# Stick-breaking attention on one core: the score product of the low key parts over 128 rows instead of 64

## The chip, the core and the metric

The kernel runs on one core of one Trainium2 chip. The time is device microseconds from start to end of one execution, lower is better. All five engines take part: TensorE (PE, with its weight loads PEld) does the matrix products, VectorE (DVE) and ScalarE (ACT) the elementwise work, GpSimd (POOL) sets memory and issues some transfers, SyncE (SP) issues most transfers.

## The reference

A small decoder trunk over 512 positions of width 1024: an S5 state-space mixer with a gated output (GLU), a gated feed-forward layer with a width-3 convolution, one shared key/value projection, a stick-breaking attention of 16 heads of 64 dimensions over those keys and values, a second feed-forward layer, and a last norm. The part that the change touches is this:

```python
def stick_breaking_attention(h, w_q, k, v, w_o):
    scale = HEAD_DIM ** -0.5
    q = (h @ w_q).reshape(...).transpose(0, 2, 1, 3) * scale
    for blk in range(seq // Q_BLOCK):
        ...
        z = jnp.einsum('bhqd,bhkd->bhqk', qb, kb).astype(jnp.float32)
        causal = s_idx < t_idx
        log_beta = jax.nn.log_sigmoid(z)
        log_one_minus = jnp.where(causal, log_beta - z, 0.0)
        rem = lax.cumsum(log_one_minus, axis=3, reverse=True) - log_one_minus
        w = jnp.where(causal, jnp.exp(log_beta + rem), 0.0)
        outs.append(jnp.einsum('bhqk,bhkd->bhqd', w, vb))
    return o @ w_o
```

## The kernel before

The trunk runs in stages, one after the other: S5 with its GLU, the first feed-forward layer, attention, the second feed-forward layer with the last norm. Activations lie with features on the 128 partitions and the 512 positions along the row. Every 32-bit operand of a large product is split into a high part that TensorE's rounded 32-bit format (fp32r) holds and a low part, the rest; a product is then three matmuls, high by high, high by low, low by high. Weights come in by DMA as raw tiles (`awr` in attention, `wvr` in the GLU), get their high part on ScalarE (`awh`, line 157) and their low part on VectorE (`awl`, line 112).

In attention the keys and queries of two heads at a time are one 128-row tile: rows 0 to 63 are the even head, rows 64 to 127 the odd head. `Proj` makes for the keys the tiles `kqa` and `kqb`, one for each head, that hold the head's high part twice (rows 0 to 63 and rows 64 to 127), and one tile `kql` with the low parts of both heads, each on its own rows. For the queries, `kqa` and `kqb` hold the high part on the head's own rows and the low part on the other 64. So the first score matmul of a block of 128 keys, `kqa` by `kqa`, sums high by high and high by low over 128 rows. The second, low keys by high queries, takes 64 rows of `kql` and of the queries: `kl[rows, kc]`, `qs[rows, q]`.

`Head.scores` goes through the key blocks 3, 1, 2, 0, which reach 128, 384, 256 and 512 queries. The scores `z` fill three PSUM banks. After the block's two matmuls a product of the identity with a mask tile adds -1e30 above the diagonal: over 256 columns after block 1 (for the diagonals of blocks 3 and 1, which share a bank), over 128 columns after blocks 2 and 0. That is 11 matmuls for a head. A head then goes on so: ScalarE makes the log terms `t`, VectorE the softplus and its split `lh`, `ll`; TensorE adds the running sums (`cumulate`: products with `cntri` and `cnones`); ScalarE exponentiates to `wh` and `w`, VectorE makes `wl` from them; TensorE multiplies by the values `vv` into `ob`.

The loop over the 16 heads is written out in the order in which PE, DVE and ACT run it (`tc.manual_schedule`): `cumulate` of head i, `scores` of head i+1, a third of the projection jobs (`kqb`, `v`, `ob` products that prepare later heads or the output), `values` of head i, then two more thirds of the jobs. Between them DVE and ACT run the splits of weights and keys. Outside the loop the scheduler of the language orders the instructions, GpSimd's for the whole program among them. Tiles come from rings: `kq` is a ring of ten tiles, five for each pair of heads, thus two pairs. Memory of closed pools is used again, and an instruction on a new tile waits for the last use of what lay there.

The convolution's coefficients of each feed-forward layer are loaded to a tile of their own (`cw`, line 818, issued by ScalarE).

Of the kernel before, what the change touches and what calls it, by code (L numbers as in the profile page):

```python
# [7 lines left out]
F32 = mybir.dt.float32  # L8
F32R = mybir.dt.float32r
# [38 lines left out]
def trunk(ctx: ExitStack, tc: tile.TileContext, A, out):  # L48
# [11 lines left out]
    class Work:  # L60
        """The work tiles [128, 512] of a phase, by tag."""

# [13 lines left out]
    def banks_by_tag(**bufs):  # L76
        """Deals the eight banks of PSUM to a phase's tags, those longest unused first."""
        ids = sorted(range(8), key=lambda i: max([n for n, u in enumerate(used) if u == i], default=-1))
        cur["p"] = {}
        for tag, n in bufs.items():  # L80
            cur["p"][tag], ids = ids[:n], ids[n:]
# [37 lines left out]

    # ------------------------------------------------------------ constants  # L120
    par = const.tile([P, 168], F32, name="par")
# [11 lines left out]

    # ------------------------------------------------------------ weights
    def load_raw(src, cols, name="w", dma=None):
# [4 lines left out]
    def load_split(src, cols, gain=None, name="w", dma=None):  # L140
        """src: a [128, cols*128] block of weights in DRAM; two parts whose sum it is exactly."""
        raw = load_raw(src, cols, name, dma)
        if gain is not None:
            i, ks = gain if isinstance(gain, tuple) else (gain, slice(0, KT))
            g = cst[:, i, ks]
            n = ks.stop - ks.start
            r3 = raw.rearrange("p (k n) -> p k n", k=n)
            tt(r3, r3, bc(g, 2, [P, n, 8 * P // n]), MUL)
        return split_w(raw, cols, name)
# [23 lines left out]

    # ------------------------------------------------------------ norms
    def split_x(k, gain, perm=False):
# [63 lines left out]

    # ------------------------------------------------------------ S5  # L240
    def s5(st_next):
        banks_by_tag(st=1, u=2, g=2, kb=1, v=1, y=1)
        with tc.tile_pool(name="s5", bufs=1) as sp, ExitStack() as wctx:
# [59 lines left out]
            def steps():  # L303
                """The steps of the tensor engine that go between the dependent ones."""
                for n in range(KT):
# [30 lines left out]
            def load(k):  # L336
                """Two steps' weights of the first of the gated outputs."""
                raw = wp.tile([P, 8 * P], F32, tag="raw", name="wvr", bufs=3)
                for i in range(0, HALVES, 2):
                    GP.dma_start(out=raw[:, i * 2 * P:(i + 2) * 2 * P].rearrange("p (h c) -> p h c", h=2),  # L340
                                 in_=A["w_glu"][i // 2, :, :, k * P:(k + 2) * P].rearrange("h p c -> p h c"))
                raws.append(raw)
# [127 lines left out]

            # powers 0..8 of A
            pw3 = L("pw3", [32, 3, 9])
# [13 lines left out]

            # the powers times f, which stands with C
            pwc3 = L("pwc3", [32, 3, 8])
# [19 lines left out]

            # unit rotations over the chunks and the decay of a chunk
            mg2 = op2(mag, mag, MUL)  # L510
# [23 lines left out]
            def rotations():  # L534
                """The rotations of the first half of the chunks, of all groups, by doubling."""
                for lv in range(5):
# [13 lines left out]
            def turn_products(n):  # L550
                """The second half of the chunks, of four pairs of groups."""
                q = T("tq", tag="tq").rearrange("p (i r q c) -> p i r q c", i=2, r=2, q=4)
# [13 lines left out]
            def products(m3, pw3, n, e0):  # L566
                """The three products of a complex multiplication by the powers from e0, of four pairs of groups."""
                pr = slice(4 * n, 4 * n + 4)
# [6 lines left out]
            def sums(o, k3):  # L575
                """Their sums: the real part and the (for C negated) imaginary part."""
                o4 = o.rearrange("p (r a c) -> p r a c", r=2, a=4)
                tt(o4, bc(k3[:, :, 0], 1, [P, 2, 4, P]), k3[:, :, 1:3].rearrange("p a t c -> p t a c"), ADD)

            def op_c(n):  # L580
                """C A^e (re, im) of four pairs of groups."""
                k3 = products(c3, pwc3, n, 0)
# [4 lines left out]
            def kk(n):  # L587
                """The within-chunk response, as a matrix from the inputs to the outputs of a chunk."""
                cmr, cmn = unit[n]["c"]
# [24 lines left out]
            def op_b(n):  # L614
                """A^(8-j) bb of four pairs of groups."""
                unit[n] = {}
# [28 lines left out]
            def decays(n):  # L645
                """The decay of a chunk, for the chunks of four pairs of groups after their first."""
                decay[n] = sp2.tile([P, 256], F32, name="mt", bufs=1)
# [4 lines left out]
            def states(n):  # L652
                """The states before each chunk: a real recurrence in the frame that turns with them."""
                pr = slice(4 * n, 4 * n + 4)
# [154 lines left out]

    # ------------------------------------------------------------ conv FFN  # L810
    def ffn(layer, prev, st_next):
# [5 lines left out]
    def ffn_body(layer, xs, rb, st_next):  # L817
        cw = const.tile([P, FT, 4], F32, name=f"cw{layer}")
        nc.scalar.dma_start(out=cw, in_=A["conv"][layer])
# [34 lines left out]

    # ------------------------------------------------------------ attention
    def attention(prev, st_next):
        with Work("att", aw=9, tw=4, os=16, o=2, kq=10, kv=2):
            banks_by_tag(z=6, d0=1, d1=1)
# [4 lines left out]
    def attention_body(ap, xs, rb, rtok, st_next):  # L863
        consts = {}

        def load_consts():
            for n, wd in (("ntri", P), ("nones", P), ("ident", P), ("mask", 2 * P)):
                raw = T("cr", tag="kv")
                nc.scalar.dma_start(out=raw[:, 0:wd], in_=A[n])
                consts[n] = t = ap.tile([P, wd], F32R, name="c" + n)  # L870
# [7 lines left out]

        # the weights, in the order of their use
        class Weight:  # L880
# [23 lines left out]
        class Proj:  # L904
            """Keys or queries of two heads."""
            halves = 2
# [14 lines left out]
            def top(self):  # L921
                """Keys: [high, high] of each head and the low parts; queries: [high, low] and [low, high]."""
                self.a, self.d = T("kqa", F32R, "kq"), T("kqb", F32R, "kq")
# [3 lines left out]
            def rest(self):  # L927
                if self.keys:
                    self.l = T("kql", F32R, "kq")
                    low = self.l[:64], self.l[64:]  # L930
                else:
# [10 lines left out]
        class Vals:  # L942
            """Values of four heads and half of the keys: [keys, block, head, hi|lo], hi and lo swapped for the odd heads."""

# [42 lines left out]
        class Out:  # L987
            """Part of the sum of one output tile, added to the trunk; its steps end at the given ks."""

# [26 lines left out]

        kq, vvs, vws = {}, {}, {}
        width = {0: 512, 1: 384, 2: 256, 3: 128}
        place = {0: (2, 0), 3: (0, 0), 1: (0, 128), 2: (1, 0)}
        banks = ((512, (3, 1)), (256, (2,)), (512, (0,)))  # L1020

        class Head:
# [11 lines left out]
            def scores(self):  # L1034
                keys, queries = kq[self.pair]
                kd, kl, qs, rows = keys[self.e], keys[2], queries[self.e], self.rows
                self.z = [B(f"z{i}", "z") for i in range(3)]
                for kb in (3, 1, 2, 0):
# [3 lines left out]
                    mm(o, kd[:, kc], qs[:, q], kb != 1, False)  # L1042
                    mm(o, kl[rows, kc], qs[rows, q], False, False)
                    if kb == 1:
                        mm(self.z[0][:, 0:2 * P], consts["ident"], consts["mask"], False, False)
                    elif kb != 3:
                        mm(o[:, 0:P], consts["ident"], consts["mask"][:, 0:P], False, False)

            def log_terms(self, between=None):
                """exp, ln of the softplus (ScalarE)."""  # L1050
                self.L = [(W2("lh", wd), W2("ll", wd)) for wd, _ in banks]
# [108 lines left out]

        # which weights are split beside which half of which job
        side = {(j, h): [] for j in range(-2, len(jobs)) for h in range(2)}

        def split_at(m, js, h):
            """Gain a half before, the high part at this half, the low part a half later."""
            p = 2 * js + h
# [166 lines left out]

    # ------------------------------------------------------------ the trunk
    class Next:
# [8 lines left out]
    class Final:  # L1344
        """The last norm: the sums of squares by a product with ones, the last tile and the output by halves."""

# [136 lines left out]
```

## Time and profile before

| | us |
|---|---|
| median of 3 runs | 1259.54 (1258.92 to 1259.91) |
| span of the profiled execution | 1258.9 |
| PE busy in it | 1231.0 (98%) |
| DVE busy | 810.5 (64%) |
| ACT busy | 541.1 (43%) |
| POOL busy | 22.1 (2%) |
| the stretch from the first score block to the end of the last running sums | 608.5 to 850.6 |

The span runs from the first to the last instruction of the profiled execution; it is 0.64 us under the median of the runs. The granted TensorE clock was 0.995 over the span. A matmul's row gives its start and its duration up to the modelled end; since matmuls overlap in the pipeline, what one costs in a stream is the time from its start to the start of the next. Line 106 is the helper that issues every matmul, so that groups are told apart by their tiles.

### The profile page before, as it was taken

How to read it: one execution, taken by the hardware profiler on the slowest of the kernel's cores; microseconds unless marked ns; L12 is line 12 of the kernel's file. 1: busy time of each engine (PE TensorE's matmuls, PEld its weight loads, DVE VectorE, ACT ScalarE, POOL GpSimd, SP SyncE). 2: the span in 40 equal slices, each digit the busy share in tenths (PEclk: the TensorE clock that was granted, in tenths of full speed). 3: DMA queues.
4: the chain of work that ended last, by engine and by line, in shares of the span. 5: the costliest groups of instructions: out<-in, count | busy, mean ns of one | idle time of the engine just before them, and what ended most of it. 6: DMA issues, size and time to landing. Idle time of an engine off the chain costs nothing.

```text
span 1258.9 us, 16218 instructions
## 1 busy us (share of the span) xinstructions
PE 1231.0 (98%) x6411; PEld 987.5 (78%) x6411; DVE 810.5 (64%) x1284; ACT 541.1 (43%) x866; POOL 22.1 (2%) x61
## 2 busy tenths in 40 slices
PE   7989999999999999999999999999999999999996
PEld 3457788788888888888888888888888888888884
DVE  7999664656445635558787878777656345535554
ACT  5235353433223323344676768665433233313331
POOL 1011010000000000000000000000000000000000
PEclk9999999999999999999999999999999999999998
DMA  5565343232233233223211211113333233233321
GB/s 202 148 171 141 102 134 97 87 100 88 97 101 96 88 101 101 97 89 111 68 51 37 65 51 47 39 51 101 101 101 91 94 100 98 88 101 98 94 73 67
DMA packets 55068, 118.54 MB, mean 94 GB/s; under 512 B 12912, under 2 KB 28528, under 8 KB 54992
## 3 DMA queue, kind: packets, MB, share of 16 engines
q1 hardware_dynamic: 50880, 105.55, 27.4%
q0 software_dynamic: 3248, 11.54, 2.9%
q8 instruction: 50, 0.82, 0.3%
q10 hardware_dynamic: 864, 0.42, 0.1%
q14 instruction: 26, 0.21, 0.1%
HBM read 109.10 MB, written 8.39 MB: 93 GB/s over the span
## 4 chain that ended last, share of the span: by engine, by line
PE 90%; DVE 8%; ACT 1%; DMA 1%; issue 1%; SPq 0%; DVEq 0%; ACTq 0%
PE fd L106 19%; PE fu L106 19%; PE fg L106 19%; PE z L106 7%; PE kqb L106 7%; PE gl L106 6%; PE ob L106 5%; PE v L106 4%; DVE k L112 2%; DVE p L112 1%; PE u L106 1%; PE y L106 1%; DVE cm L112 1%; DVE u L112 1%; DVE rv L670 1%
## 5 line engine op out<-in xcount | busy, mean ns | idle before, releaser
L106 PE MATMUL fd<-ah,wdh 128*128 128x512 f32 (+1 forms) x359 | 140.5, 391 | 0.0
L106 PE MATMUL fd<-ah,wdl 128*128 128x512 f32 (+1 forms) x359 | 139.2, 388 | 0.0
L106 PE MATMUL fd<-al,wdh 128*128 128x512 f32 (+1 forms) x359 | 137.8, 384 | 0.0
L112 DVE TENSOR_TENSOR x<-x,fd 128x512 f32<-128x512 f32 (+1 forms) x49 | 33.1, 676 | 119.8 <-PE fd L106 119.8
L157 ACT CAST wuh<-wur 128x1024 fp32r<-128x1024 f32 x44 | 46.4, 1054 | 134.4 <-PE fg L106 118.0
L157 ACT CAST wdh<-wdr 128x896 fp32r<-128x896 f32 (+1 forms) x48 | 47.2, 983 | 127.9 <-PE fd L106 98.1
L112 DVE TENSOR_TENSOR g<-fg,rb 128x512 f32<-128x512 f32 x44 | 30.4, 692 | 96.2 <-PE fg L106 93.5
L106 PE MATMUL fu<-xh,wuh 128*128 128x512 f32 x220 | 86.0, 391 | 0.0
L106 PE MATMUL fg<-xh,wgl 128*128 128x512 f32 x220 | 85.8, 390 | 0.0
L106 PE MATMUL fg<-xh,wgh 128*128 128x512 f32 x220 | 85.7, 390 | 0.0
L106 PE MATMUL fu<-xh,wul 128*128 128x512 f32 x220 | 85.6, 389 | 0.0
L106 PE MATMUL fg<-xl,wgh 128*128 128x512 f32 x220 | 85.6, 389 | 0.0
L106 PE MATMUL fu<-xl,wuh 128*128 128x512 f32 x220 | 85.6, 389 | 0.0
L112 DVE TENSOR_TENSOR u<-fu,rb 128x512 f32<-128x512 f32 x44 | 30.4, 692 | 80.5 <-PE fu L106 80.5
L106 PE MATMUL fu<-xhl,wuh 128*128 128x512 f32 x264 | 81.9, 391 | 0.0
L106 PE MATMUL fg<-xhl,wgh 128*128 128x512 f32 x264 | 81.5, 389 | 0.0
L106 PEld LDWEIGHTS fd<-ah,wdl 128*128 128x128 f32 x359 | 67.4, 188 | 15.2
L106 PEld LDWEIGHTS fd<-al,wdh 128*128 128x128 f32 x359 | 67.4, 188 | 14.8 <-issue 0.2
L106 PEld LDWEIGHTS fd<-ah,wdh 128*128 128x128 f32 x359 | 67.5, 188 | 13.3 <-issue 0.2
L157 ACT CAST wgh<-wgr 128x1024 fp32r<-128x1024 f32 x44 | 46.4, 1054 | 71.0 <-PE fd L106 33.0
L106 PE MATMUL u<-xg,wi 128*128 128x512 f32 x128 | 63.4, 628 | 7.8 <-ACT xg L270 7.8
L109 DVE SCALAR_TENSOR_TENSOR acc<-g,cw,acc 128x511 f32<-128x511 f32 x88 | 65.8, 748 | 2.4 <-ACT acc L832 0.9
(246 smaller groups left out, 2813.1 us busy)
## 6 DMA issues: line engine op xcount, KB each, us to landing
wgr<-in_w_up SPq DMA_DIRECT2D x44, 512.0 KB, 3.5
wur<-in_w_up SPq DMA_DIRECT2D x44, 512.0 KB, 3.5
wdr<-in_w_dn SPq DMA_DIRECT2D x32, 448.0 KB, 3.2
wdr<-in_w_dn SPq DMA_DIRECT2D x16, 512.0 KB, 3.4
wvr<-in_w_glu POOLq DMA_DIRECT2D x12, 512.0 KB, 3.8
ks<-kx SPq DMA_DIRECT2D x32, 128.0 KB, 2.4
m<-ks SPq DMA_DIRECT2D x8, 512.0 KB, 4.1
awr<-in_w_k SPq DMA_DIRECT2D x8, 512.0 KB, 3.5
```

The costliest lines, as they stand in the source:

```text
L106: PE.matmul(o, lhsT=lhsT, rhs=rhs, start=start, stop=stop, skip_group_check=True)
L109: (eng or V).scalar_tensor_tensor(out=o, in0=a, scalar=s, in1=b, op0=op0, op1=op1)
L112: (eng or V).tensor_tensor(out=o, in0=a, in1=b, op=op)
L157: SC.copy(out=hi, in_=raw)
L670: V.tensor_tensor_scan(out=rv[:, c], data0=decay[n], data1=wv[:, c], initial=0.0, op0=MUL, op1=ADD)
```

## The change

The low parts of the keys no longer lie together in one tile of the ring. There are four tiles for the whole stage, `kl00`, `kl01`, `kl10`, `kl11` (128 rows by 512): for two alternating pairs of heads, one tile for each head. Of each tile the head's own 64 rows are written anew for each pair, as before; the other 64 rows are set to zero once, by GpSimd. The second score matmul takes all 128 rows of that tile and of the head's query tile, so that the other rows add nothing. The ring `kq` shrinks from ten tiles to eight. The mask tile is 128 wide instead of 256, and the product over 256 columns reads it twice through an access pattern with a step of zero. The convolution's coefficients of both layers share one buffer. Comments and descriptions in the source are taken out.

```diff
-        cw = const.tile([P, FT, 4], F32, name=f"cw{layer}")
+        cw = const.tile([P, FT, 4], F32, name="cw")
...
-        with Work("att", aw=9, tw=4, os=16, o=2, kq=10, kv=2):
+        with Work("att", aw=9, tw=4, os=16, o=2, kq=8, kv=2):
...
-            for n, wd in (("ntri", P), ("nones", P), ("ident", P), ("mask", 2 * P)):
+            for n, wd in (("ntri", P), ("nones", P), ("ident", P), ("mask", P)):
                 raw = T("cr", tag="kv")
-                nc.scalar.dma_start(out=raw[:, 0:wd], in_=A[n])
+                nc.scalar.dma_start(out=raw[:, 0:wd], in_=A[n][:, 0:wd])
...
                 if self.keys:
-                    self.l = T("kql", F32R, "kq")
-                    low = self.l[:64], self.l[64:]
+                    self.l = lows[self.pair % 2]
+                    low = self.l[0][:64], self.l[1][64:]
...
+        lows = []
+        for i in range(2):
+            pair = [ap.tile([P, S], F32R, name=f"kl{i}{e}") for e in range(2)]
+            for e, t in enumerate(pair):
+                GP.memset(t[64 - 64 * e:128 - 64 * e].bitcast(F32), 0.0)
+            lows.append(pair)
...
-                kd, kl, qs, rows = keys[self.e], keys[2], queries[self.e], self.rows
+                kd, kl, qs = keys[self.e], keys[2][self.e], queries[self.e]
...
                     mm(o, kd[:, kc], qs[:, q], kb != 1, False)
-                    mm(o, kl[rows, kc], qs[rows, q], False, False)
+                    mm(o, kl[:, kc], qs[:, q], False, False)
                     if kb == 1:
-                        mm(self.z[0][:, 0:2 * P], consts["ident"], consts["mask"], False, False)
+                        mm(self.z[0][:, 0:2 * P].rearrange("p (b q) -> p b q", b=2), consts["ident"],
+                           bc(consts["mask"], 1, [P, 2, P]), False, False)
                     elif kb != 3:
-                        mm(o[:, 0:P], consts["ident"], consts["mask"][:, 0:P], False, False)
+                        mm(o[:, 0:P], consts["ident"], consts["mask"], False, False)
```

On PE the order stays. These are the first matmuls of the score block of the second head (the odd one, so that its high keys are `kqb`; sizes are those of the output), before:

```order
L106 MATMUL z_5113<-kqb 128x128
L106 MATMUL z_5113<-kqb,kql 128x128
L106 MATMUL z_5113<-kqb 128x384
L106 MATMUL z_5113<-kqb,kql 128x384
L106 MATMUL z_5113<-cmask,cident 128x256
```

The same place after:

```order
L106 MATMUL z_5119<-kqb 128x128
L106 MATMUL z_5119<-kqb,kl_4763 128x128
L106 MATMUL z_5119<-kqb 128x384
L106 MATMUL z_5119<-kqb,kl_4763 128x384
L106 MATMUL z_5119<-cmask,cident 128x256
```

No matmul has moved; the low keys come from the head's own tile, and the row count of the products, which these rows don't show, is 128 throughout.

On POOL the four instructions that set zeros stand at the end of the S5 stage, between transfers of the GLU's weights (`wvr`); `mt` and `xv` are small tiles of S5:

```order
 L650 MEMSET mt 128x4
 L680 MEMSET xv 128x8
-L137 DMA wvr<-in_w_glu 128x1024 x11
+L137 DMA wvr<-in_w_glu 128x1024
+L1023 MEMSET kl_4762 64x512
+L1023 MEMSET kl_4763 64x512
+L1023 MEMSET kl_4766 64x512
+L1023 MEMSET kl_4767 64x512
+L137 DMA wvr<-in_w_glu 128x1024 x10
```

Ten weight transfers now stand behind the zeros in POOL's queue. By the program's semaphores the first of the four waits for the last use of the memory that the tiles are laid over, on PE the product `yt<-yh,nid` of the last S5 round.

On ACT the load of the second layer's coefficients was the third instruction of the program and now stands near the end of the first feed-forward layer, right after its last Silu (`s<-acc`, line 836).

## The prediction

> **What bounds the kernel now.** I read the page first: the engines' busy time and the chain of work that ended last.
>
> ```profile
> PE 1231.0 (98%) x6411; PEld 987.5 (78%) x6411; DVE 810.5 (64%) x1284; ACT 541.1 (43%) x866; POOL 22.1 (2%) x61
> PE 90%; DVE 8%; ACT 1%; DMA 1%; issue 1%; SPq 0%; DVEq 0%; ACTq 0%
> ```
>
> TensorE carries 90% of the chain. Then the chain in order of time (start, length, what), for the attention stage: its first score block, the running sums and score block of one head, and the running sums of the last head, which has no score block behind it.
>
> ```profile
> 608.53 3.02 PE z L106 x11
> ...
> 622.82 5.68 PE z L106 x29
> ...
> 632.55 5.46 PE kqb L106 x24
> ...
> 658.91 2.92 PE v L106 x24
> ...
> 847.96 2.65 PE z L106 x18
> ```
>
> Between 608.5 and 850.6 the chain is PE alone, one piece after the other without a gap, so in this stage any time that PE saves is saved in the end, until another engine is late. A score block of 11 matmuls takes 3.02 us; 5.68 less 2.65 gives 3.03 for the next one.
>
> Is 3.02 us much for its work? The stream rates are in the same rows: 24 matmuls of 512 columns in 5.46 us, 0.2275 each; 24 of 256 columns in 2.92, 0.1217 each. The timeline of PE (start, duration, what) shows the running sums and then the score block of one head matmul by matmul. The step from start to start is the cost:
>
> ```profile
> 638.08 0.68 PE L106 MATMUL z<-lh,cnones 128*128 128x128 f32 x4
> 638.60 0.40 PE L106 MATMUL z<-ll,cntri 128*128 128x512 f32 x1
> ...
> 640.52 0.22 PE L106 MATMUL z<-kqa 128*128 128x128 f32 x1
> 640.67 0.32 PE L106 MATMUL z<-kqa,kql 64*128 64x128 f32 x1
> 640.92 0.44 PE L106 MATMUL z<-kqa 128*128 128x384 f32 x1
> 641.29 0.43 PE L106 MATMUL z<-kqa,kql 64*128 64x384 f32 x1
> 641.65 0.39 PE L106 MATMUL z<-cmask,cident 128*128 128x256 f32 x1
> 641.88 0.28 PE L106 MATMUL z<-kqa 128*128 128x256 f32 x1
> 642.09 0.38 PE L106 MATMUL z<-kqa,kql 64*128 64x256 f32 x1
> 642.40 0.33 PE L106 MATMUL z<-cmask,cident 128*128 128x128 f32 x1
> 642.56 0.44 PE L106 MATMUL z<-kqa 128*128 128x512 f32 x1
> 642.93 0.50 PE L106 MATMUL z<-kqa,kql 64*128 64x512 f32 x1
> 643.36 0.33 PE L106 MATMUL z<-cmask,cident 128*128 128x128 f32 x1
> 643.53 0.45 PE L106 MATMUL kqb<-xh,awh 128*128 128x512 f32 x1
> 643.81 0.40 PE L106 MATMUL kqb<-xl,awh 128*128 128x512 f32 x1
> ```
>
> The sign to read is 64*128 against 128*128. Every step from a 128-row matmul to a 64-row one and back is long: 0.37 for 512 columns ahead of the switch and 0.43 after it, where 0.2275 is the stream; 0.25 for 128 columns of `kql`. Even the products behind a switch back run late, the mask's (0.23 for 256 columns) and the first `kqb` (0.28). There are eight switches in a block. The running sums just ahead change weights and widths as often, without one switch, and stay near the stream: the four rows merged at 638.08 (three of 128 columns, one of 384) take 0.52, so that at 0.171 for the 384 (three quarters of 0.2275) a 128-column one costs 0.117.
>
> **The change part by part.** The same 11 matmuls stay, all with 128 rows. At the rates above: four of 128 columns at 0.117 (0.468), three of 256 at 0.1217 (0.365), two of 384 at 0.171 (0.342), two of 512 at 0.2275 (0.455), together 1.63 us. Saved per head: 3.02 - 1.63 = 1.39, and 0.05 on the first product behind the block (0.28 against 0.2275), 1.44 in all; times 16 heads, 23.0 us. All of it is on the chain. Two bounds: a block may run at the pure column rate, 3072 columns in 1.36 us, which saves 1.71 a head or 27.4 us; or the extra of the switches may stay whole, which saves nothing. I take 23.0, since the running sums have the same mix of widths.
>
> The TensorE page of the Trainium skill ("TensorE: Matmul & The Clock Gate", Part 3) says that matmuls with few rows overlap when they use distinct row groups, so by it half-height products are the ones to keep; its price is worked out among the rivals. Here each 64-row product stands between two of 128 rows, which use all groups, and the steps above show no overlap.
>
> What is late next? DVE and ACT work for the next head while PE runs on. Their load by stretch of one head (length, then PE, PEld, DVE, ACT, POOL, clock, DMA): the first and the last of the five in which DVE is busy for 13.5 us or more, and one between.
>
> ```profile
> 653.20:668.90 15.70, 15.70 (x111) 14.08 (x110) 13.60 (x22) 11.19 (x23) 0.00 (x0) 1.00 0.22 68
> 684.20:699.40 15.20, 15.20 (x74) 12.16 (x74) 13.56 (x22) 12.44 (x24) 0.00 (x0) 1.00 0.23 71
> 776.00:791.60 15.60, 15.60 (x110) 14.00 (x109) 13.51 (x22) 11.08 (x23) 0.00 (x0) 1.00 0.20 60
> ```
>
> A stretch of 15.20 becomes 13.76, just over DVE's 13.56. The tightest hand-over inside one is that of `wl`, which hangs on the running sums ahead of the score block and is read by the value products behind it:
>
> ```profile
> 690.68 1.62 DVE L112 TENSOR_TENSOR wl<-w,wh 128x512 fp32r<-128x512 f32 x3
> 693.53 0.39 PE L106 MATMUL ob<-wl,vv 128*128 128x512 f32 x1
> 693.50 0.69 DVE L109 SCALAR_TENSOR_TENSOR t<-z,t 128x512 f32<-128x512 f32 x1 [1.20 <-ACT t L1060]
> ```
>
> The last `wl` ends at 692.30 and is read at 693.53, a slack of 1.23; 1.44 less leaves PE waiting 0.21. I charge 0.21 to each of the five heavy stretches, 1 us. DVE's own wait of 1.20 for the log terms says that DVE isn't out of time there. Net gain 22.0.
>
> The zeros: POOL's four MEMSETs of 512 columns. Nearest rows:
>
> ```profile
> 2.47 0.97 POOL L496 MEMSET bdr<- 128x1024 f32 x1
> 3.36 0.97 POOL L497 MEMSET bdi<- 128x1024 f32 x1
> ...
> 151.06 0.53 POOL L137 DMA_DIRECT2D wvr<-in_w_glu  x1 [7.33 <-DVE wvl L112]
> 159.08 0.53 POOL L137 DMA_DIRECT2D wvr<-in_w_glu  x1 [7.49 <-DVE wvl L112]
> ```
>
> ```profile
> 156.31 0.40 PE L106 MATMUL yt<-yh,nid 128*128 128x512 f32 x1
> ```
>
> From start to start 1024 columns take 0.89, so 512 take 0.45 and four 1.8. They may start when `yt<-yh,nid` ends at 156.71 and are over near 158.6, before the next transfer, which VectorE holds back until 159.08 anyway. Cost nothing. If that cover is gone, the ten transfers behind slip, and their own slack is next:
>
> ```profile
> L157 ACT CAST wvh<-wvr x19: 404/1051/1057, 87.1 to 209.8; 128x1024 fp32r<-128x1024 f32 x15, 128x256 fp32r<-128x256 f32 x4
> L137 POOL DMA_DIRECT2D wvr<-in_w_glu x16: 528/528/549, 103.8 to 196.0; - x16
> DMA to landing us min/median/max: 2.9/3.7/5.3
> ```
>
> The last one is issued at 196.0, lands 3.7 later, and its first reader, the cast, starts at 209.8: ten microseconds of cover there. From below: zeros remove no work, so no gain.
>
> The coefficients: one DMA issue less at the start of ACT and one more (0.4) near 549.8, where ACT idles:
>
> ```profile
> L819 ACTq DMA_DIRECT2D cw<-in_conv x2: 401/426/450, 0.8 to 1.2; - x2
> ```
>
> ```profile
> 549.18 0.63 ACT L836 ACTIVATE s<-acc 128x512 f32<-128x512 f32 x1 [1.84 <-DVE acc L109]
> 551.01 0.94 ACT L157 CAST wdh<-wdr 128x896 fp32r<-128x896 f32 x1 [1.19 <-PE fu L106]
> ```
>
> The idle 1.19 hides it, and the second layer reads them 300 us later; nothing either way.
>
> The mask: the narrower load and cast stand ahead of the loop and off the chain. The read with a step of zero has no row. From below it costs its columns, 0.1217, as taken. From above I take the slowest 128-row product on the page, full 32-bit, two records for one product:
>
> ```profile
> L106 PE MATMUL u<-xg,wi 128*128 128x512 f32 x128 | 63.4, 628 | 7.8 <-ACT xg L270 7.8
> ```
>
> 64 products in 63.4 us are 0.99 for 512 columns, 0.50 for 256: 0.38 more a head, 6 us. I take the lower end, since the columns read are of the same type and count as in the row it is nearest to, `cmask` at 641.65.
>
> The ring of eight tiles holds four for each of two pairs, as ten held five: no new wait. DVE writes as many low parts as before, on 64 rows each.
>
> Sum: 1259.54 - 22.0 = 1237.5. Against the profiled execution's own span of 1258.9, 0.6 below the median, it reads 1236.9.
>
> **The rivals.**
> VectorE sets the pace: if DVE's waits (1.20 of the 1.64 us that it idles in the stretch at 684.20) can't shrink, the five heavy stretches keep their length and lose 1.44 each, 7.2. The gain falls from 23.0 to 15.8: 1243.7. For it speaks that 13.76 leaves DVE only 0.2 us; against it that the wait is for ACT, which moves forward with the scores.
>
> No floor for narrow products: the block at the column rate, and no waits: 1259.5 - 27.4 = 1232.1. Against it: 0.117 in the running sums.
>
> The switch is not the cause, but the change of weights and widths: the extra stays and the time is 1259.5. Against it stands the row of running sums at 638.08. The tiling page ("TensorEngine Tiling (Array Packing)", Key Properties, of the Trainium skill) says that a change of tiling mode drains the array; by it this rival falls, and the long steps at 64*128 agree.
>
> Slower: half-height products run beside a neighbour now, so that their columns are free, and full-height ones can't. Each head would pay its 1280 columns of low products, 0.57 us, 9.1 in all: 1268.6. It decides if a `kql` step costs under its stream of 0.057 to 0.2275; the rows show 0.25 to 0.43. The rule named above is this one's only support.
>
> **How the numbers follow.** Chances: forecast 0.78 (own range 1233 to 1241, which holds waits of 0 to 4 us more or less), pace of VectorE 0.10, no floor 0.06, switch not the cause 0.04, slower 0.02. The range 1232 to 1244 holds the forecast, the mask's upper bound (1243.5) and the two cases beside them, VectorE's and the one with no floor, which are its ends; the last two stay out, 0.06. A change of 0.2% (2.5 us) is about what a measurement of this kernel tells from none: faster 0.95, same 0.03, slower 0.02.
>
> **What would show it.** Right: the second score products read 128*128, the pieces `z x29` of the chain shrink from 5.68 to about 4.3, the first from 3.02 to 1.6; mask products step by 0.12; POOL's transfer stays at 159.1; and PE waits in attention sum to a microsecond or so, for `wl` or an evacuation. Wrong: steps still near 0.37 and 0.43 at 128 rows, a mask step near 0.5, PE idle before `ob<-wl` or `z<-lh` of a microsecond in each heavy stretch, or the GLU's weights late.

## The result, and the profile after

The changed kernel takes 1237.63 us (median of four runs, 1236.96 to 1240.25) against 1259.72 for the one before, a ratio of 0.983 (0.981 to 0.984). The forecast was 1237.5.

The page of the changed kernel, engines and chain, to be set beside the first fence of the prediction:

```profile
PE 1207.6 (98%) x6411; PEld 982.8 (80%) x6411; DVE 809.6 (66%) x1284; ACT 539.3 (44%) x866; POOL 24.2 (2%) x65
PE 89%; DVE 8%; ACT 1%; issue 1%; DMA 1%; SPq 0%; DVEq 0%; ACTq 0%
```

PE is busy 23.4 us less with as many matmuls; VectorE and ScalarE do what they did, within 2 us, and POOL's 2.1 more are the zeros. The chain in order of time, attention stage:

```profile
606.83 1.58 PE z L106 x11
...
619.68 4.23 PE z L106 x29
...
824.24 2.64 PE z L106 x18
```

The first score block takes 1.58 where it took 3.02, running sums and block together 4.23 where they took 5.68, and the running sums alone are as they were. The stage runs from 606.83 to 826.88, 220.05 us against 242.08: 22.0 less. (It begins 1.7 us earlier than in the profile before. In the profiles of those experiments that leave the feed-forward matmuls as they are it begins anywhere between 607.0 and 608.7, at 608.28 in two that are built on the changed kernel, so that this is no part of the change.)

The block of the same head as in the prediction, on PE and its weight loads (start, duration, engine, what):

```profile
635.98 0.22 PE L106 MATMUL z<-kqa 128*128 128x128 f32 x1
635.98 0.19 PEld L106 LDWEIGHTS z<-kqa,kl 128*128 128x128 f32 x1
636.04 0.27 PE L106 MATMUL z<-kqa,kl 128*128 128x128 f32 x1
...
636.38 0.34 PE L106 MATMUL z<-kqa,kl 128*128 128x384 f32 x1
...
636.55 0.28 PE L106 MATMUL z<-cmask,cident 128*128 128x256 f32 x1
...
636.67 0.28 PE L106 MATMUL z<-kqa 128*128 128x256 f32 x1
...
636.91 0.22 PE L106 MATMUL z<-cmask,cident 128*128 128x128 f32 x1
636.91 0.19 PEld L106 LDWEIGHTS z<-kqa 128*128 128x128 f32 x1
636.97 0.45 PE L106 MATMUL z<-kqa 128*128 128x512 f32 x1
...
637.25 0.39 PE L106 MATMUL z<-kqa,kl 128*128 128x512 f32 x1
...
637.48 0.22 PE L106 MATMUL z<-cmask,cident 128*128 128x128 f32 x1
...
637.54 0.45 PE L106 MATMUL kqb<-xh,awh 128*128 128x512 f32 x1
...
637.83 0.40 PE L106 MATMUL kqb<-xl,awh 128*128 128x512 f32 x1
```

All products read 128*128. The weights of `kl` start to load at 635.98 together with the product ahead of theirs. Two rows of the kernel before at the same place show what a change of row count does to that:

```profile
640.52 0.22 PE L106 MATMUL z<-kqa 128*128 128x128 f32 x1
640.67 0.18 PEld L106 LDWEIGHTS z<-kqa,kql 64*128 64x128 f32 x1 [0.20 <-issue]
640.67 0.32 PE L106 MATMUL z<-kqa,kql 64*128 64x128 f32 x1
```

There the load starts 0.15 us after the product ahead has started, at the same time as its own matmul. It is so at all eight changes of that block. So in these traces no weights are loaded ahead at a change of row count. The waits of PEld in the stage, before and then after (who waited for whom, us, times, longest):

```profile
PEld z L106 <- issue: 16.6, 79, 0.2
```

```profile
PEld ob L106 <- DVE wl L112: 0.7, 2, 0.4
PEld kqb L106 <- DVE kq L109: 0.5, 2, 0.3
```

16.6 us in which weight loads waited for nothing that the profile shows are gone, and 1.2 us of waiting for VectorE has come.

### The profile page after: what moved, and what is told of

Same layout as the page of the kernel before. It is cut to its first block, busy times and chain, and to the rows that moved or that the text cites. A ratio compares the mean times of both kernels' runs of the same rounds, so it can differ in the third digit from the quotient of the medians.

```text
span 1235.2 us, 16227 instructions
## 1 busy us (share of the span) xinstructions
PE 1207.6 (98%) x6411; PEld 982.8 (80%) x6411; DVE 809.6 (66%) x1284; ACT 539.3 (44%) x866; POOL 24.2 (2%) x65
## 4 chain that ended last, share of the span: by engine, by line
PE 89%; DVE 8%; ACT 1%; issue 1%; DMA 1%; SPq 0%; DVEq 0%; ACTq 0%
PE fd L106 20%; PE fu L106 19%; PE fg L106 19%; PE kqb L106 7%; PE gl L106 6%; PE z L106 5%; PE ob L106 5%; PE v L106 4%; DVE k L112 2%; DVE p L112 1%; PE u L106 1%; PE y L106 1%; DVE cm L112 1%; DVE u L112 1%; DVE rv L670 1%
```

## The experiments

The theory: what cost time was the change between 64-row and 128-row matmuls, eight in a score block, and not the 64-row product itself, the widths, or the small edits.

**The small edits alone.** The kernel before, with

```diff
-            for n, wd in (("ntri", P), ("nones", P), ("ident", P), ("mask", 2 * P)):
+            for n, wd in (("ntri", P), ("nones", P), ("ident", P), ("mask", P)):
...
-        cw = const.tile([P, FT, 4], F32, name=f"cw{layer}")
+        cw = const.tile([P, FT, 4], F32, name="cw")
```

and the mask read twice, as in the change.

> The kernel before with only the small edits: the mask tile 128 wide and read twice, the coefficients of both layers in one buffer; the second score product keeps its 64 rows. Theory (the cost is the change between 64 and 128 rows, and all of the gain comes from taking it away): the time of before, 1259.7 within 1.5 us, and score blocks of 3.02 us. Rival (the small edits carry part of the gain): 2 us or more under before.

Measured: 1259.85 against 1259.83 us, ratio 0.9997 (0.9988 to 1.0006), score blocks of 3.02 us as before. The small edits carry nothing. The opposite part, the zero rows without the small edits, can't be had: the four new tiles then leave the attention stage 0.6 KB per partition short of memory. Room for them is all that the edits give.

**Fewer changes with the same products.** The kernel before, in another order:

```diff
                 for kb in (3, 1, 2, 0):
                     ...
                     mm(o, kd[:, kc], qs[:, q], kb != 1, False)
+                for kb in (3, 1, 2, 0):
+                    ...
                     mm(o, kl[rows, kc], qs[rows, q], False, False)
-                    if kb == 1:
+                for kb in (1, 2, 0):
+                    ...
+                    if kb == 1:
                         mm(self.z[0][:, 0:2 * P], consts["ident"], consts["mask"], False, False)
```

> The kernel before with the products of a score block in another order: the four high products of 128 rows, then the four low products of 64 rows, then the three mask products. Rows, columns and number of products are those of before; the changes of row count fall from eight to two a head. Theory (each change costs): a block falls from 3.02 by about six eighths of 1.46 to about 1.9 us, the time to about 1242.5 (1240 to 1246). Rival (a 64-row product is slow in itself, 0.14 to 0.2 us over its columns): four slow products stay, the block keeps 2.3 us or more and the time 1248 or more.

Measured: 1243.77 us, ratio 0.987 (0.986 to 0.989), a gain of 16.1. The timeline of PE, equal products merged:

```profile
639.09 0.80 PE L106 MATMUL z<-kqa 128*128 128x128 f32 x4
639.82 0.90 PE L106 MATMUL z<-kqa,kql 64*128 64x128 f32 x4
640.65 0.56 PE L106 MATMUL z<-cmask,cident 128*128 128x256 f32 x3
641.05 0.45 PE L106 MATMUL kqb<-xh,awh 128*128 128x512 f32 x1
```

The block takes 1.96 (639.09 to 641.05). The four 64-row products with their 1280 columns (0.57 at the stream rate) take 0.83, a quarter of a microsecond over it once and not four times. The rival, slow 64-row products, falls.

The same order with 128 rows, to see what order alone does:

> The changed kernel in the order of the grouped experiment: four high products, four low products of 128 rows, then the three mask products. No change of row count. Theory: order alone costs or saves only the weight loads that narrow products don't cover, under 0.1 us a head: 1236 to 1239. Rival (the order, not the rows, makes the gain of the grouped experiment): 3 us or more under the changed kernel.

Measured: 1238.58 us, ratio 0.983 (0.982 to 0.985), a microsecond over the changed kernel and inside its spread. Its block:

```profile
637.97 0.80 PE L106 MATMUL z<-kqa 128*128 128x128 f32 x4
638.61 0.80 PE L106 MATMUL z<-kqa,kl 128*128 128x128 f32 x4
639.25 0.45 PE L106 MATMUL z<-cmask,cident 128*128 128x256 f32 x3
639.53 0.45 PE L106 MATMUL kqb<-xh,awh 128*128 128x512 f32 x1
```

1.56 against 1.96: one pair of changes costs 0.40 us. (Else the two kernels differ only in where the low keys lie and in the small edits, which carry nothing.) Group by group, the high products take 0.73 against 0.64, the low ones 0.83 against 0.64 and the mask's 0.40 against 0.28, so 0.09 falls ahead of the first change, 0.19 between the two, and 0.12 behind the second.

**One pair left in the changed kernel.**

```diff
-                    mm(o, kl[:, kc], qs[:, q], False, False)
+                    r = self.rows if kb == 0 else slice(0, P)
+                    mm(o, kl[r, kc], qs[r, q], False, False)
```

> The changed kernel, but the widest key block (512 queries) keeps 64 rows in its second product: two changes of row count a head. Theory: by the steps of the two traces (0.37 against 0.28 ahead, 0.43 against 0.23 in it, 0.165 against 0.06 behind) 0.40 us a head, 6.4 us in all, less what VectorE's waits of 1.2 us take up: 1242.5 to 1244. Rival (the cost goes with the 64-row columns, of which this block has 512 of 1280): 0.4 of 22, 1246.5.

Measured: 1243.44 us, ratio 0.987 (0.985 to 0.989); 5.8 over the changed kernel. The chain's pieces of running sums and block read 4.62 against 4.23, 0.39 a pair:

```profile
635.66 4.62 PE z L106 x29
```

Sixteen of these are 6.2, less the 1.2 us of waits for VectorE, which this trace no longer has: the stage runs from 608.28 to 833.47, 5.1 longer. The price doesn't follow the columns.

**The same cost put where there was none.** In the changed kernel's feed-forward layers, gate and up products, fifth of eight steps (the code is shortened):

```diff
             mm(bank, hi[:, c], xh, ...)
-            mm(bank, hi[:, c], xl, False, False)
+            mm(bank, hi[:64, c], xl[:64], False, False)
             mm(bank, lo[:, c], xh, ...)
```

> The changed kernel with a switch put where there was none: in each of the 88 gate and up products of the two feed-forward layers (24 matmuls of 512 columns each), the middle one of the fifth of the eight steps takes 64 rows instead of 128, so that half of one low part is left out of the sum. Theory (a change of row count costs by itself, in any stage that PE bounds): two changes for each product; by the wide steps of the score block, 0.37 ahead and 0.43 at 64 rows against 0.2275, 0.35 us a pair, up to 0.45 if the product behind is late too: 31 to 40 us more than the changed kernel, 1268 to 1277, though there is less to compute. Rival (the cost belongs to the score block, to its banks or its waits): no more than 2 us over 1237.6.

Measured: 1272.07 us, 34.4 over the changed kernel, 0.39 for each of the 88 pairs; ratio to the kernel before 1.010 (1.008 to 1.011). The 24 matmuls of a product take 5.84 where they took 5.44. Half of one matmul in 24 was left out, and the kernel lost all that the change had gained and 12 us more. One of the places:

```profile
299.93 0.39 PE L106 MATMUL fg<-xh,wgh 128*128 128x512 f32 x1
300.25 0.50 PE L106 MATMUL fg<-xl,wgh 64*128 64x512 f32 x1
300.67 0.50 PE L106 MATMUL fg<-xh,wgl 128*128 128x512 f32 x1
301.01 0.61 PE L106 MATMUL fg<-xhl,wgh 128*128 128x512 f32 x2
```

Against 0.2275 the step into the 64-row product is 0.09 longer, the one out of it 0.19, and the next 0.11: the parts of the 0.39, and nearly those of the score block.

With all three products of that step at 64 rows:

> As the run with one 64-row matmul in each gate and up product, but all three matmuls of the fifth step take 64 rows, so that half of that step is left out of the sum; the changes of row count stay two for each product. Theory (the price is that of a change): the same time as with one, within 3 us. Rival (a 64-row matmul is slow in itself): three times the loss, 93 to 120 us over the changed kernel.

Measured: 1275.65 us, ratio 1.013 (1.011 to 1.014), 3.6 over the run with one, where 3 at most was expected: 0.43 a place instead of 0.39, with three times as many 64-row products. So two more of them add 0.04 and not twice 0.39; nearly all of the price is that of the change. Between the 64-row products the weights are loaded ahead again: a load starts at 300.91 for the matmul at 301.14.

**Do two row groups overlap?** As the run with one 64-row product, and behind it a second one, on the other 64 rows and into another bank (the code is shortened)

```diff
+            mm(scr, hi[64:, c], xl[64:], True, True)
```

> As the run with one 64-row matmul in each gate and up product, and right behind it a second one with the other 64 rows into another bank that nobody reads (its half is still left out of the sum). No more changes of row count than with one, but four. If products in distinct row groups overlap, the time of the run with one, within 1 us. If they don't, 0.2275 us more for each of 88, 20 us more. No theory on the result hangs on it; it tests the rule weighed in the prediction.

Measured: 1275.59 us, ratio 1.013 (1.011 to 1.014), 3.5 over the run without it: more than the 1 us that was expected if the two overlap, and far from the 20 us if they don't. That is 0.04 for each and not 0.2275. The trace:

```profile
301.28 0.50 PE L106 MATMUL fg<-xl,wgh 64*128 64x512 f32 x1
...
301.28 0.50 PE L106 MATMUL scr<-xl,wgh 64*128 64x512 f32 x1
...
301.71 0.19 PEld L106 LDWEIGHTS fg<-xh,wgl 128*128 128x128 f32 x1 [0.25 <-issue]
```

Both start at 301.28. The rule of the Trainium skill's page "TensorE: Matmul & The Clock Gate" (Part 3) that products in distinct row groups run side by side is true here, at some 0.04 us. It was no argument for the kernel before, where a 64-row product never stood beside another of the other group.

**How much slack is left on VectorE?** The last term of the forecast was PE's wait for VectorE. In the changed kernel:

```diff
-X = (2, 1, 0)
+X = (1, 1, 1)
```

This sets how many weight steps VectorE takes at each of three places in a head.

> The changed kernel with one weight step (a gain or a low part, 1.22 us of VectorE) of each head moved from ahead of the low parts wl to the later third of the head (X = 1, 1, 1 instead of 2, 1, 0). Theory (what the gain still lacks is PE's wait for VectorE's wl, 0.7 us in two heads): that wait goes, other waits of the order of 0.5 us stay or come, the time is 0 to 1 us under the changed kernel. Rival (VectorE has no slack left): a wait of the same size at another place, and 1238 or more.

Measured: 1256.61 us, 19.0 over the changed kernel; ratio to the kernel before 0.998 (0.997 to 0.999). The theory of this run was wrong, and `wl` was later, not sooner:

```profile
ACT awh L157 <- DVE awr L112: 17.5, 5, 3.5
PEld ob L106 <- DVE wl L112: 9.7, 13, 1.2
...
DVE awl L112 <- ACT awh L157: 7.4, 8, 1.2
```

Fewer gains (`awr`) are done ahead, so ScalarE's cast `awh` waits for VectorE (17.5 us where it was 7.0), and VectorE's next step `awl` for the cast (7.4 where it was 0.5), with `wl` behind it. In the changed kernel a head leaves VectorE (third of the busy times) little room for such stalls. A lighter head and the tightest one:

```profile
634.30:648.20 13.90, 13.90 (x76) 12.07 (x75) 12.42 (x22) 12.12 (x23) 0.00 (x0) 1.00 0.13 39
689.53:703.41 13.88, 13.88 (x74) 11.87 (x74) 13.55 (x23) 12.47 (x24) 0.00 (x0) 1.00 0.12 40
```

Not all of the 19.0 is waiting. PE's weight loads wait 17.5 us for VectorE and ScalarE, against 1.2 in the changed kernel. Besides, in this run the granted clock (last figure but two in the first row) dips behind some of the longest waits:

```profile
660.00:670.00 10.00, 10.00 (x71) 9.83 (x70) 8.19 (x16) 6.10 (x13) 0.00 (x0) 0.86 0.08 14
660.11 0.41 PE L106 MATMUL v<-awl,xh 128*128 128x256 f32 x1
660.32 0.41 PE L106 MATMUL v<-awh,xl 128*128 128x256 f32 x1
```

There 256 columns step by 0.21, where 0.12 is the stream. The slice before reads 0.97, and a second dip reads 0.93 and 0.90 (760 to 780). Over these four slices of 10 us that is some 3.4 us, an estimate from the clock that is missing. What makes the clock dip stays open: from 700 to 730 PE stands still for longer, and the clock holds.

To tell a bad order from short heads, the same in the kernel before:

> The kernel before with the same reordering of VectorE's weight steps (X = 1, 1, 1) that cost the changed kernel 19 us. Theory (the shorter heads took VectorE's slack: 13.9 us of head for 12.1 to 13.5 us of work, where it was 15.3): the kernel before has 1.4 us more room in each head and loses less than half of that, 0 to 8 us, with PE waiting for wl 5 us or less. Rival (the order is bad in itself, whatever the length of a head): about 19 us here too, 1278.

Measured: 1266.80 us, ratio 1.006 (1.004 to 1.007): 7.3 lost where the short heads lose 19.0, and PE waits half as long for `wl`:

```profile
PEld ob L106 <- DVE wl L112: 4.6, 6, 1.2
```

With that order the change gains 10 us instead of 22. Some 3 of the missing 12 are the clock's, which in this run stays at 1.00 through the stage. So the rival "VectorE sets the pace" is near: the gain is whole only as long as VectorE's order has no stall in it.

## Why the prediction was right

- *The block shrinks by the extra of the switches.* Right. Forecast 1.63 us from 3.02, came 1.56 (635.98 to 637.54); over the 16 heads 15 times 1.45 (5.68 to 4.23) and once 1.44, 23.2 us, where 23.0 stood in the sum.
- *0.05 more on the first product behind the block.* Wrong, and hidden in the sum. That product takes 0.29 (637.54 to 637.83) as before, 0.28, so it has nothing to do with the switch. The narrow mask ahead of it steps by 0.06, and the next weights only start to load with the mask and take 0.19. The same shows at 636.97 to 637.25 inside the block. The prediction gave a narrow product 0.117, with its lateness; the trace puts the lateness on the product behind it: 128 columns step by 0.06 (0.11 for the second of two in a row), and the 512 behind them by 0.28 where the prediction had 0.2275. So the block came out 0.07 shorter than forecast and the product behind it 0.06 longer; the two together are 1.85 where the forecast had 1.86.
- *Waits of 1 us for VectorE.* The size was right, 1.2, and in part by luck: five waits of 0.21 for `wl` were forecast, and four came, two for `wl` (0.7) and two for the evacuation `kq` (0.5). The rival that VectorE's own waits can't shrink falls: the tightest head takes 13.88 (13.76 was forecast without the wait), and VectorE idles 0.33 in it, where it idled 1.64.
- *The zeros are hidden.* Right, with nothing left over:

```profile
154.57 0.40 PE L106 MATMUL yt<-yh,nid 128*128 128x512 f32 x1
...
155.08 2.24 POOL L1023 MEMSET kl<- 64x512 f32 x4 [5.24 <-PE yt L106]
...
157.34 0.53 POOL L137 DMA_DIRECT2D wvr<-in_w_glu  x1
```

  They take 2.24, not 1.8, and end as the next transfer is due: it leaves 2.77 us after the start of `yt<-yh,nid`, as it did before (156.31 and 159.08).
- *The mask's second read costs its columns.* Right, 0.12 for 256 (636.55 to 636.67), and the run with the small edits alone shows no loss. *The coefficients cost nothing.* Right by the same run.
- The sum: 23.2 less 1.2 is 22.0, the stage's 22.0 and the 22.1 of the medians.

That the array drains at a change of mode, as the tiling page of the Trainium skill says ("TensorEngine Tiling (Array Packing)", Key Properties), agrees with the late weight loads; the page has no price, the runs have 0.36 (eight in a block, 1.45 over four pairs) to 0.43 us a pair.

What stays open: whether the 0.09 ahead of a 64-row product is the drain and the 0.19 and 0.11 behind it the weight loads that could not start early. The traces show when the loads start, not why.

## What to carry to other kernels

Look in the timeline for a row count that changes between neighbours (64*128 beside 128*128): each pair of changes cost 0.4 us here whatever the product, as much as nearly two products of 512 columns. Fill the unused rows with zeros once and keep all products full, or put the half-height ones together, which gives most of it (16 of 22 us here) for nothing but an order. Before counting such a gain, add up the engine that runs beside: here the heads shrank to just above VectorE's work, 13.88 us against 13.55 in the tightest, and with another order of its steps the change gains 10 us instead of 22.

## What was not expected of the hardware

A second 64-row product in the other row group cost 0.04 us beside the first, so the second of such a pair comes nearly free; the changes around the pair still cost their 0.39. And a narrow product passes its lateness on: 128 columns step by 0.06 us, but the 512 columns behind them by 0.28 in place of 0.2275; their weights begin to load only with the narrow one.
